# A fused transformer layer on one core: the parts of a block sum in another order, and the casts of a weight pair one quad at a time

## The chip, the cores and the metric

The kernel runs on one core of a Trainium2 chip. The metric is the device time of one execution in microseconds (us); of several runs the median is taken. A measurement of this kernel tells changes of about 0.3% (some 5.5 us) from none.

## The reference, cut to what matters

One layer of a hybrid decoder for 256 positions of width 2048 in float32: a half-step feed-forward block, a mixing block (differential attention beside an mLSTM, with one combined input projection and one output projection), a second half-step feed-forward block, and a final norm. Most of the work is in the feed-forward blocks (inner width 5632):

```
def swiglu(h, w_gate, w_up, w_down):
    return (jax.nn.silu(h @ w_gate) * (h @ w_up)) @ w_down

x = x + 0.5 * swiglu(rmsnorm(x, ffn1_norm[l]), ffn1_w_gate[l], ffn1_w_up[l], ffn1_w_down[l])
...   # h @ w_in, attention and mLSTM, concat @ w_out
x = x + 0.5 * swiglu(rmsnorm(x, ffn2_norm[l]), ffn2_w_gate[l], ffn2_w_up[l], ffn2_w_down[l])
return rmsnorm(x, final_norm)
```

## The kernel before, in words

**A product in three.** A float32 operand is split into a high part, a cast to a rounded format by ScalarE (ACT, line 131, tiles `wh`), and a low part, the difference, by VectorE (DVE, line 132, tiles `wl`). A product of two operands is three matmuls on TensorE (PE): line 180 and line 181 take the weights' high part with the high and the low part of the other operand, line 183 takes the low part `wl`. `mms` issues lines 180 and 181 for all its jobs first and line 183 after them, so `wl` may be a little later than `wh`. `wh` and `wl` have four buffers each.

**Quads.** `Paired` computes two column chunks (512 columns each) of a linear layer at a time, for the two halves of 128 positions. For `ns` of its 2x2 blocks of weights, called quads, it takes seven products instead of eight, by sums of weight blocks and of input blocks. For the rest of the depth it takes plain products (`plain`, tiles `rawp`). Quads are loaded and split two at a time, as pairs of 128x1024 elements; `twos` is the list of them. With `ns` of 5 it is the first pair (quads 0 and 1), the second pair (quads 2 and 3), and a single quad (4), of 128x512 elements. The gate and up projections have `ns` of 5 in 20 passes: 9 in the first feed-forward block, 11 in the second. All other passes have `ns` of 2, 3 or 4, where the list has one pair, a pair and a single quad, or two pairs.

**The stages of a pass.** `leading` loads a pair (POOL's DMA queue, lines 433 and 207; the first passes on SP's), takes the first products (A1), adds weight blocks in place on DVE (line 463), and takes the products with the second sum (S1). Behind S1, `second_sum` adds slot 2 of the raw tile to slot 0: for the pairs by an accumulating DMA from POOL's queue (line 478), for the last entry of the list, the single quad, by DVE (line 480). Between the steps of `leading` run the last steps (`third`) of the pass before. Then `sums` does for each entry of the list the products with the third sum (S2, line 508) from slot 0, loads another block (`late`, SP's queue, line 494), adds that block to slot 0 by an accumulating DMA (line 512, POOL), and takes the block's own products (`bare`, line 500) one entry behind. Behind the last S2, ACT copies the accumulator (`us`, line 486) and DVE subtracts it from another one (line 517). Then come the products with slot 1 (S3, line 523), and in `second` plain products mixed with `both`, which uses slots 0 and 2 of each quad. The order on the engines is that in which the code issues, with loads and splits moved ahead by a priority of 400 instructions (`AHEAD`); copies and additions that empty accumulators are put among the splits by `ahead_of_splits`.

**The output projection.** Its first pass runs with `gently`. In `leading`, after each pair, `flush(1)` issues one piece of pending work; here these are transposes of the mixer's outputs (`y_transposes`, line 1075, which read `yb` or `ya`).

Of the kernel before, what the change touches and what calls it, by code (L numbers as in the profile page):

```python
# [9 lines left out]
F32 = mybir.dt.float32  # L10
# [3 lines left out]
ALU = mybir.AluOpType  # L14
# [45 lines left out]
def tile_trunk_layer(ctx: ExitStack, tc: tile.TileContext, x, xt, par, bias_if, lamv, fnorm,  # L60
                     wg1, wu1, wd1, wqk0, wqk1, wqk2, win, wout, wg2, wu2, wd2, out):
    nc = tc.nc
# [33 lines left out]
    def seeded(which):  # L96
        return ps_acc.tile([P, CW], F32, tag=f"acc{which}", name=nm(f"acc{which}"), bufs=1)
# [26 lines left out]
    def split_gain(src, gcol, hi, lo):  # L124
# [2 lines left out]
        nc.vector.scalar_tensor_tensor(lo, src, prm[:, gcol:gcol + 1], hi.bitcast(F32),  # L127
                                       op0=ALU.mult, op1=ALU.subtract)

    def split(src, hi, lo):  # L130
        return (nc.scalar.copy(hi, src),  # L131
                nc.vector.tensor_tensor(out=lo, in0=src, in1=hi.bitcast(F32), op=ALU.subtract))  # L132

    splits, queued = [], ([], [])

    def after(late, early):

        tc.add_manual_dep(late.ins, early.ins.name,  # L140
                          mybir.DependencyInfo(mybir.DependencyClass.NoSync, mybir.DependencyReason.DATA),
                          reason="order")

    def ahead_of_splits(i, ins, slack=SLACK):
        queued[i].append((len(splits) + slack, ins))

    ahead = ([], [])

    def split_weights(src, hi, lo):
        made = split(src, hi, lo)  # L150
        for late, q, past in zip(made, queued, ahead):
            while q and len(splits) >= q[0][0]:
                past.append(q.pop(0)[1])
            del past[:-3]
            for early in past:
                after(late, early)
        return made


    def pair_tiles(pool, tag, shape):  # L160
        return (pool.tile(shape, F32R, tag=tag + "h", name=nm(tag + "h")),
                pool.tile(shape, F32R, tag=tag + "l", name=nm(tag + "l")))
# [11 lines left out]
    newest = []  # L174

    def mms(jobs):


        for acc, lh, ll, rh, rl, first, last, on in jobs:
            nc.tensor.matmul(acc, lh, rh, start=first, stop=False, skip_group_check=on)  # L180
            nc.tensor.matmul(acc, ll, rh, start=False, stop=False, skip_group_check=on)  # L181
        for acc, lh, ll, rh, rl, first, last, on in jobs:
            newest[:] = [nc.tensor.matmul(acc, lh, rl, start=False, stop=last, skip_group_check=on)]  # L183
# [15 lines left out]
    def flush(n=None):  # L199

        now = pending[:n]
        del pending[:n]
        for f in now:
            f()
# [87 lines left out]
    def chunk_to_xt(c, gbase, xp, ns, now=KD):  # L292


        def run(j):
            tr = ps_tr.tile([P, 2, S], F32, tag="tr", name=nm("tr"))
            for i in range(2):
                for hb in range(NT):
                    nc.tensor.transpose(tr[:, i, hb * P:(hb + 1) * P],
                                        xres[:, hb, (2 * j + i) * P:(2 * j + i + 1) * P], ident)  # L300
            with tc.high_priority(offset=AHEAD):
                if j < ns:
                    sum_pair(xp, j, gained(tr, prm[:, gbase + 2 * j:gbase + 2 * j + 2]), j >= now)
                else:
                    hi, lo = plain_pair(xp, j)
                    for i in range(2):
                        split_gain(tr[:, i, :], gbase + 2 * j + i, hi[:, i, :], lo[:, i, :])

        pending.extend(functools.partial(run, j) for j in (2 * c, 2 * c + 1))
# [14 lines left out]
    def sum_pair(xp, j, g, put_off=False):  # L324
        hi, lo = sum_tiles(xp, j)
        split(g, hi[:, 0:4, :], lo[:, 0:4, :])
        (side.append if put_off else lambda f: f())(functools.partial(sums, g, hi, lo))

    def sums(g, hi, lo):
        s = wk("xsum").rearrange("p (a b) -> p a b", b=P)  # L330
        tt = nc.vector.tensor_tensor
        tt(out=s[:, 0:2, :], in0=g[:, 0:2, :], in1=g[:, 1:4:2, :], op=ALU.subtract)
        tt(out=s[:, 2, :], in0=s[:, 1, :], in1=g[:, 0, :], op=ALU.subtract)
        tt(out=s[:, 3, :], in0=g[:, 2, :], in1=s[:, 2, :], op=ALU.add)
        split(s, hi[:, 4:8, :], lo[:, 4:8, :])
# [18 lines left out]
    def hid_transposes(hs, hid, c, ns):  # L354
        def run(j):
            tr = ps_tr.tile([P, 2, S], F32, tag="tr", name=nm("tr"))
            for i in range(2):
                for hb in range(NT):
                    k = (2 * j + i) % 4
                    nc.tensor.transpose(tr[:, i, hb * P:(hb + 1) * P], hs[hb][:, k * P:(k + 1) * P], ident)  # L360
            if j < ns:
                g = wk("hg")
                act.copy(g, tr.rearrange("p a b -> p (a b)"))
                with tc.high_priority(offset=AHEAD):
                    sum_pair(hid, j, g.rearrange("p (a b) -> p a b", b=P), True)
            else:
                with tc.high_priority(offset=AHEAD):
                    split(tr, *plain_pair(hid, j))

        pending.extend(functools.partial(run, j) for j in (2 * c, 2 * c + 1))  # L370

    def wk(name):
        return work.tile([P, CW], F32, tag="w", name=nm(name))
# [11 lines left out]
    def soon(extra=40):  # L385
        return tc.high_priority(offset=AHEAD + extra)
# [17 lines left out]
    def aside(work):  # L404

        if work:
            work.pop(0)()

    class Paired:
# [28 lines left out]
            self.raws.extend(raw[:, q, :, :] for q in range(len(js)))  # L438
            return raw

        def split_two(self, src):
            with tc.high_priority(offset=AHEAD):
                t = [x[:, 0:src.shape[1], :] for x in pair_tiles(wsp, "w", [P, 2, self.n])]
                splits.append(split_weights(src, *t))
            return t

        def part(self, js, acc, xi, slot, first=False, last=False):

            t = self.split_two(self.twin[js[0]][:, :, slot, :])
            mms([self.job(acc, j, xi, t, i, first and j == 0, last and j == self.ns - 1, not first)  # L450
                 for i, j in enumerate(js)])

# [49 lines left out]
        def sums(self):  # L502

            ds = self.copied(self.d, wk("ds"))
            lates = []
            for js in self.twos:
                lates.append((js, self.late(js)))
                self.part(js, self.x, S2, 0)
                if self.rest[0] // UK not in self.xp:
                    flush(1)  # L510
                with tc.high_priority(offset=AHEAD):
                    nc.gpsimd.dma_start(self.twin[js[0]][:, :, 0, :], lates[-1][1][:, 0:len(js), :],  # L512
                                        accum_op=ALU.add)
                if js[-1] == self.ns - 1:
                    us = self.copied(self.x, wk("us"))
                    with soon():
                        ahead_of_splits(1, nc.vector.tensor_tensor(out=self.d, in0=self.d, in1=us, op=ALU.subtract))
                if len(lates) > 1:
                    self.bare(*lates.pop(0))
            for js, raw in lates:  # L520
                self.bare(js, raw)
            for js in self.twos:
                self.part(js, self.x, S3, 1)
            self.n21 = self.copied(self.x, seeded(N21), SLACK - 2)
            with soon():
                ahead_of_splits(1, nc.vector.tensor_tensor(out=self.x, in0=ds, in1=self.x, op=ALU.subtract))
# [52 lines left out]
    class Chain:  # L579
# [7 lines left out]
        def run(self, p, half, end, last_units=1, gently=False):  # L587

            done = 0
            q = len(p.twos)  # L590
            first = p.leading()
            for i in range(q):
                while done < min(self.steps - 1, -(-(i + 1) * self.steps // (q + 1))):
                    next(self.stream)
                    done += 1
                next(first)
                flush(1)
                aside(side)
            while done < self.steps - 1:
                next(self.stream)  # L600
                done += 1
            next(first, None)
            while done < self.steps:
                next(self.stream)
                done += 1
            self.end()
            p.sums()
            half(p.second(gently))
            self.put(p.third(last_units), len(p.rest), lambda: end(p.accs()))
# [257 lines left out]
    late = {}  # L867
# [263 lines left out]
    for c in (0, 2):  # L1131
        chain.run(Paired(yT, wout[c], wout[c + 1], KD, NP_OUT), functools.partial(finish_out, c),
                  functools.partial(finish_out, c + 1),
                  gently=not c)
# [108 lines left out]
```

## Time and profile before

| what | value |
|---|---|
| median of 3 runs | 1851.19 us (1849.18 to 1855.7) |
| the profiled execution | 1848.02 us, its span 1846.3 us |
| busy in the span | PE 1785.6 us (97%), DVE 1588.7 (86%), ACT 1232.9 (67%), POOL 340.0 (18%) |
| mean granted clock of TensorE | 0.991 |
| traffic | 427.00 MB, 231 GB/s in the mean |

The span runs from the first to the last instruction; the execution's own time is 1.7 us more. A row of the waits reads: who waited, for whom, us in total, times, the longest. A row of the timeline reads: start, duration, engine, line, operation, out<-in, count, and in brackets the engine's idle time before it and what ended it. Matmuls are pipelined: each is shown 0.39 us long where one starts every 0.2275 us.

### The profile page before, as it was taken

The numbers are of one execution on the slowest core, as the hardware profiler recorded it, in microseconds if no ns is written. First come the engines' busy times: TensorE is split into PE (matmuls) and PEld (weight loads), VectorE is DVE, ScalarE is ACT, GpSimd is POOL, SyncE is SP. The second block draws the span as 40 slices with busy tenths as digits, with TensorE's granted clock in tenths as the row PEclk, the third lists the DMA queues.
The fourth block names the chain that finished last, engine by engine and source line by source line (L and its number), as shares of the span: only waits on it lengthen the run. The fifth ranks groups of instructions, "written<-read, shape, count | busy, mean of one in ns | idle before, by whom it ended". The sixth has DMA issues, their size and how long they took to land. (4 is left out here: it accounts for less than half of the span.)

```text
span 1846.3 us, 23318 instructions
## 1 busy us (share of the span) xinstructions
PE 1785.6 (97%) x7942; PEld 1442.7 (78%) x7942; DVE 1588.7 (86%) x1871; ACT 1232.9 (67%) x1659; POOL 340.0 (18%) x444
## 2 busy tenths in 40 slices
PE   9999999999999999999999999999999899999998
PEld 7887777777777788987887887777777677777776
DVE  7888898798888989896788998988898698888988
ACT  7666666566666668776676676675666566666665
POOL 0011221222122211111111001122222222122210
PEclk9999999999999999999999999999999899999999
DMA  9788997888799876576766678887987788798874
GB/s 341 246 240 220 254 266 218 232 260 249 215 238 265 240 246 201 184 227 194 217 193 195 200 211 234 243 240 230 260 253 212 195 258 252 221 238 250 244 242 126
DMA packets 150423, 427.00 MB, mean 231 GB/s; under 512 B 14528, under 2 KB 15600, under 8 KB 150048
## 3 DMA queue, kind: packets, MB, share of 16 engines
q0 software_dynamic: 71472, 191.67, 42.4%
q1 hardware_dynamic: 77680, 231.76, 36.6%
q10 hardware_dynamic: 1152, 2.09, 0.3%
q8 instruction: 62, 1.02, 0.2%
q14 instruction: 57, 0.47, 0.1%
HBM read 349.56 MB, written 2.10 MB: 190 GB/s over the span
## 5 line engine op out<-in xcount | busy, mean ns | idle before, releaser
L131 ACT CAST wh<-raw 128x1024 fp32r<-128x1024 f32 (+1 forms) x593 | 555.4, 943 | 388.2 <-DVE raw L463 94.8
L132 DVE TENSOR_TENSOR wl<-raw,wh 128x1024 fp32r<-128x1024 f32 (+1 forms) x593 | 636.9, 1085 | 181.6 <-ACT wh L131 177.2
L180 PE MATMUL acc<-wh,xs 128*128 128x512 f32 (+2 forms) x924 | 363.9, 394 | 34.0 <-ACT wh L131 33.9
L132 DVE TENSOR_TENSOR wl<-rawp,wh 128x1024 fp32r<-128x1024 f32 (+3 forms) x316 | 373.5, 1195 | 26.6 <-ACT wh L131 22.4
L131 ACT CAST wh<-rawp 128x1024 fp32r<-128x1024 f32 (+3 forms) x316 | 323.2, 1033 | 62.0 <-PE acc L181 34.5
L181 PE MATMUL acc<-wh,xs 128*128 128x512 f32 (+2 forms) x924 | 359.4, 389 | 0.0
L183 PE MATMUL acc<-wl,xs 128*128 128x512 f32 (+2 forms) x924 | 312.0, 394 | 6.9 <-DVE wl L132 5.7
L180 PEld LDWEIGHTS acc<-wh,xs 128*128 128x128 f32 x924 | 175.0, 189 | 79.7 <-ACT wh L131 45.0
L180 PE MATMUL acc<-wh,xt 128*128 128x512 f32 (+2 forms) x592 | 228.6, 387 | 0.0
L181 PE MATMUL acc<-wh,xt 128*128 128x512 f32 (+2 forms) x592 | 228.0, 386 | 0.0
L180 PE MATMUL accn<-wh,xt 128*128 128x512 f32 (+1 forms) x576 | 227.3, 398 | 0.7 <-ACT wh L131 0.6
L181 PE MATMUL accn<-wh,xt 128*128 128x512 f32 (+1 forms) x576 | 224.1, 392 | 0.7
L183 PEld LDWEIGHTS acc<-wl,xs 128*128 128x128 f32 x924 | 171.6, 189 | 55.3 <-DVE wl L132 22.3
L463 DVE TENSOR_TENSOR raw<-raw 128x1024 f32<-128x1024 f32 (+1 forms) x172 | 204.0, 1216 | 7.7 <-DMA raw<-in_wd_dram 6.0
L512 POOL DMA_DIRECT2D raw<-late x104 | 113.9, 1160 | 478.7 <-DVE wl L132 404.4
L181 PEld LDWEIGHTS acc<-wh,xs 128*128 128x128 f32 x924 | 175.1, 190 | 34.0
L183 PE MATMUL acc<-wl,xt 128*128 128x512 f32 (+2 forms) x592 | 165.1, 387 | 3.7 <-DVE wl L132 3.7
L183 PE MATMUL accn<-wl,xt 128*128 128x512 f32 (+1 forms) x576 | 162.0, 389 | 0.2
L180 PE MATMUL accn<-wh,xs 128*128 128x512 f32 (+1 forms) x392 | 155.1, 397 | 1.5 <-ACT wh L131 1.5
L181 PE MATMUL accn<-wh,xs 128*128 128x512 f32 (+1 forms) x392 | 154.0, 394 | 0.0
L183 PE MATMUL accn<-wl,xs 128*128 128x512 f32 (+1 forms) x392 | 139.1, 398 | 2.0 <-DVE wl L132 0.7
L183 PEld LDWEIGHTS acc<-wl,xt 128*128 128x128 f32 x592 | 109.8, 188 | 27.7 <-DVE wl L132 6.2
(229 smaller groups left out, 2052.8 us busy)
## 6 DMA issues: line engine op xcount, KB each, us to landing
rawp<-in_wd_dram SPq DMA_DIRECT2D x88, 512.0 KB, 5.6
raw<-in_wu_dram POOLq DMA_DIRECT2D x80, 512.0 KB, 8.2
rawp<-in_wu_dram SPq DMA_DIRECT2D x74, 512.0 KB, 5.1
rawp<-in_wg_dram SPq DMA_DIRECT2D x70, 512.0 KB, 6.0
raw<-late POOLq DMA_DIRECT2D x67, 512.0 KB, 5.9
raw<-in_wd_dram POOLq DMA_DIRECT2D x60, 512.0 KB, 6.8
rawp<-in_win_dram SPq DMA_DIRECT2D x44, 512.0 KB, 5.0
raw<-raw POOLq DMA_DIRECT2D x43, 512.0 KB, 5.9
```

What stands on the lines that cost most here:

```text
L131: return (nc.scalar.copy(hi, src), nc.vector.tensor_tensor(out=lo, in0=src, in1=hi.bitcast(F32), op=ALU.subtract))
L132: nc.vector.tensor_tensor(out=lo, in0=src, in1=hi.bitcast(F32), op=ALU.subtract))
L180: nc.tensor.matmul(acc, lh, rh, start=first, stop=False, skip_group_check=on)
L181: nc.tensor.matmul(acc, ll, rh, start=False, stop=False, skip_group_check=on)
L183: newest[:] = [nc.tensor.matmul(acc, lh, rl, start=False, stop=last, skip_group_check=on)]
L463: nc.vector.tensor_tensor(out=raw[:, 0:2, :], in0=raw[:, 0:3:2, :], in1=raw[:, 1:2, :].to_broadcast([P, 2, n]), op=ALU.add)
L512: nc.gpsimd.dma_start(self.twin[js[0]][:, :, 0, :], lates[-1][1][:, 0:len(js), :], accum_op=ALU.add)
```

## The change: order and casts

Four edits. In `sums` the list is walked in the order first pair, single quad, second pair; the bare products stay one entry behind, so they come as first pair, single quad, second pair too. For lists of one or two entries the order is what it was. In `part`, that is, for the pairs of A1, S1, S2 and S3, ACT casts a pair in two instructions of one quad each, and DVE still subtracts it in one; single quads, plain units, bare products and `both` are split as before. In the first pass of the output projection, `flush(1)` in `leading` is ordered behind the newest matmul.

```diff
+    def lo_part(src, hi, lo):
+        return nc.vector.tensor_tensor(out=lo, in0=src, in1=hi.bitcast(F32), op=ALU.subtract)
...
-    def split_weights(src, hi, lo):
-        made = split(src, hi, lo)
-        for late, q, past in zip(made, queued, ahead):
+    def split_weights(src, hi, lo, apart=False):
+        first = [nc.scalar.copy(hi[:, q, :], src[:, q, :]) for q in range(src.shape[1])] if apart else []
+        made = (first[-1], lo_part(src, hi, lo)) if apart else split(src, hi, lo)
+        for late, q, past in zip(first[:-1] + list(made), [queued[0]] * len(first[:-1]) + list(queued),
+                                 [ahead[0]] * len(first[:-1]) + list(ahead)):
...
         def part(self, js, acc, xi, slot, first=False, last=False):
-            t = self.split_two(self.twin[js[0]][:, :, slot, :])
+            t = self.split_two(self.twin[js[0]][:, :, slot, :], True)
...
-            for js in self.twos:
+            order = self.twos[:1] + self.twos[2:] + self.twos[1:2]
+            for js in order:
                 lates.append((js, self.late(js)))
                 self.part(js, self.x, S2, 0)
...
-                if js[-1] == self.ns - 1:
+                if js == order[-1]:
...
                 next(first)
-                flush(1)
+                if gently:
+                    with tc.issue_after(newest[0].ins):
+                        flush(1)
+                else:
+                    flush(1)
```

More of the change, by code (lines that the diff above doesn't have):

```diff
@@ L128, in split_gain @@
                                        op0=ALU.mult, op1=ALU.subtract)
+    def lo_part(src, hi, lo):
+        return nc.vector.tensor_tensor(out=lo, in0=src, in1=hi.bitcast(F32), op=ALU.subtract)
     def split(src, hi, lo):
-        return (nc.scalar.copy(hi, src),
-                nc.vector.tensor_tensor(out=lo, in0=src, in1=hi.bitcast(F32), op=ALU.subtract))
+        return nc.scalar.copy(hi, src), lo_part(src, hi, lo)
     splits, queued = [], ([], [])
@@ L439, in load, with split_two @@
             return raw
-        def split_two(self, src):
+        def split_two(self, src, apart=False):
             with tc.high_priority(offset=AHEAD):
                 t = [x[:, 0:src.shape[1], :] for x in pair_tiles(wsp, "w", [P, 2, self.n])]
-                splits.append(split_weights(src, *t))
+                splits.append(split_weights(src, *t, apart))
             return t
         def part(self, js, acc, xi, slot, first=False, last=False):
-            t = self.split_two(self.twin[js[0]][:, :, slot, :])
+            t = self.split_two(self.twin[js[0]][:, :, slot, :], True)
             mms([self.job(acc, j, xi, t, i, first and j == 0, last and j == self.ns - 1, not first)
```

## The prediction

> **What bounds the kernel now.** I read the page's first part, then the waits, then the timeline of one pass on each engine, then the stretches of all passes.
>
> ```profile
> span 1846.3 us, 23318 instructions
> PE 1785.6 (97%) x7942; PEld 1442.7 (78%) x7942; DVE 1588.7 (86%) x1871; ACT 1232.9 (67%) x1659; POOL 340.0 (18%) x444
> ```
>
> PE is busy for 97% of the span, so only its idle time, slow starts and lowered clock can be won. DVE, at 86%, is not far behind. The waits say what PE waits for:
>
> ```profile
> PE acc L180 <- ACT wh L131: 33.9, 23, 3.3
> PE acc L183 <- DVE wl L132: 9.4, 14, 1.4
> ACT wh L131 <- DMA raw<-raw: 76.0, 23, 5.5
> DVE wl L132 <- ACT wh L131: 201.6, 179, 5.8
> ```
>
> PE waits 23 times for a cast, and ACT waits 23 times for `raw<-raw`, the accumulating DMA of line 478. One pass shows that these are the same event. PE, around the third sum (S2):
>
> ```profile
> 429.57 0.39 PE L180 MATMUL acc<-wh,xs 128*128 128x512 f32 x1
> ...
> 430.48 0.61 PE L183 MATMUL acc<-wl,xs 128*128 128x512 f32 x2
> 432.75 0.50 PE L180 MATMUL acc<-wh,xs 128*128 128x512 f32 x1 [1.66 <-ACT wh L131]
> ...
> 434.58 0.39 PE L180 MATMUL accn<-wh,xs 128*128 128x512 f32 x1
> ...
> 436.38 0.39 PE L180 MATMUL acc<-wh,xs 128*128 128x512 f32 x1
> ...
> 442.29 0.39 PE L183 MATMUL acc<-wl,xs 128*128 128x512 f32 x1
> ```
>
> From 429.57 to 430.48 four matmuls start: one each 0.2275 us, so a pair (six) takes 1.365 and a single quad 0.68. The first pair's S2 ends at 430.93 (430.48 and two more starts). The second pair's S2 starts at 432.75, 1.82 late; its six take 1.83 (0.47 too long), the six bare ones behind it 1.80 (0.43 too long). This pass loses 2.72 us. ACT, POOL and SP in the same place:
>
> ```profile
> 427.24 0.57 ACT L486 COPY ds<-acc 128x512 f32<-128x512 f32 x1
> 431.66 1.04 ACT L131 CAST wh<-raw 128x1024 fp32r<-128x1024 f32 x1 [3.84 <-DMA raw<-raw]
> ...
> 433.57 0.61 ACT L131 CAST wh<-raw 128x512 fp32r<-128x512 f32 x1
> 434.08 1.56 ACT L131 CAST wh<-late 128x1024 fp32r<-128x1024 f32 x2
> ```
> ```profile
> 425.63 1.21 POOL L478 DMA_DIRECT2D raw<-raw  x1 [4.07 <-DVE wl L132]
> ```
> ```profile
> 400.18 13.15 SPq L494 DMA_DIRECT2D late<-in_wg_dram  x3
> ```
>
> POOL issues the second pair's sum at 425.63, as soon as DVE is through with S1 of that pair; it lands 6.0 later, at 431.66. ACT has been idle for 3.84 and casts; PE follows. The single quad's cast (433.57) stands in the queue behind, though its sum is made by DVE and needs no DMA. Line 480 in the next view has made it by 427.73:
>
> ```profile
> 427.04 0.69 DVE L480 TENSOR_TENSOR raw<-raw 128x512 f32<-128x512 f32 x1
> 427.64 1.22 DVE L132 TENSOR_TENSOR wl<-raw,wh 128x1024 fp32r<-128x1024 f32 x1
> 428.78 0.74 DVE L382 SCALAR_TENSOR_TENSOR sg<-acc,rstd,sg 128x512 f32<-128x512 f32 x1
> 432.73 1.23 DVE L132 TENSOR_TENSOR wl<-raw,wh 128x1024 fp32r<-128x1024 f32 x1 [3.21 <-ACT wh L131]
> 433.88 0.75 DVE L382 SCALAR_TENSOR_TENSOR sg<-acc,rstd,sg 128x512 f32<-128x512 f32 x1
> 434.54 1.22 DVE L132 TENSOR_TENSOR wl<-late,wh 128x1024 fp32r<-128x1024 f32 x1
> 435.67 0.69 DVE L132 TENSOR_TENSOR wl<-raw,wh 128x512 fp32r<-128x512 f32 x1
> ...
> 438.01 1.22 DVE L132 TENSOR_TENSOR wl<-raw,wh 128x1024 fp32r<-128x1024 f32 x1
> 439.14 0.69 DVE L517 TENSOR_TENSOR acc<-acc,us 128x512 f32<-128x512 f32 x1
> 439.74 1.22 DVE L132 TENSOR_TENSOR wl<-raw,wh 128x1024 fp32r<-128x1024 f32 x1
> ```
>
> DVE too is idle for 3.21 and then works without a gap to the end of S3: behind the stall DVE sets the pace, and this limits the gain. A pair costs it 1.13 (434.54 to 435.67), a single quad 0.60. All 20 passes with five quads have this place; one of them, the first, has no wait. For the other 19, PE in the 8 us behind the first pair's S2, one stretch each (first, some of the middle, last, and the sum over 19):
>
> ```profile
> 209.21:217.21 8.00, 6.58 (x26) 1.00 1.00 180
> ...
> 430.93:438.93 8.00, 6.14 (x25) 1.00 0.93 184
> ...
> 1353.68:1361.68 8.00, 6.30 (x20) 0.79 0.93 187
> 1449.88:1457.88 8.00, 4.84 (x12) 0.67 0.76 146
> ...
> 1691.12:1699.12 8.00, 6.14 (x19) 0.79 0.93 186
> 1736.25:1744.25 8.00, 6.28 (x20) 0.79 0.94 188
> sum 152.00, PE 121.55; mean PE 6.40
> ```
>
> The columns are length, PE busy, matmuls, granted clock, DMA share, GB/s. Idle: 152.00 - 121.55 = 30.5 us. At 430.93 the idle part is 1.86 of the 2.72 lost; the other 0.86 are starts further apart. I take 0.82 for the mean (two passes wait less): 19 x 0.82 = 15.5. The clock: 8 x 0.21 in three stretches and 8 x 0.33 in one, 7.7. Together the place costs **53.7 us**.
>
> On the clock the Trainium skill (TensorE: Matmul & The Clock Gate, HAM oscillation) says that it halves after an idle window of about 3.4 us. By that rule only the pass at 1449.88 (3.16 idle) could lose clock here, the 7.7 would mostly have other causes, and the sum below would be some 5 smaller. The stretches at 1353.68, 1691.12 and 1736.25, with 1.7 to 1.9 idle in 8 us and 0.79 granted, speak against the rule as the only cause.
>
> **The change part by part.**
>
> *The order.* In the pass above, ACT is free at 427.81. It casts the single quad (0.51 to the next start, from 433.57 to 434.08) and the first pair's bare block by 429.4; their buffers were freed by S1. The late blocks are long there: SP issued three by 413.3. Moving the single quad ahead moves its late load and its accumulating DMA ahead of the second pair's on SP and POOL too. The second pair's late block becomes the third load; with the 6.0 of the sum's DMA it lands by 419.5, and its first user is behind 433. On POOL the single quad's issue takes 1.2 in a queue that then waits for the second pair's DVE anyway, and slot 0 is not read again before `both`, beyond S3 (442.5). I cost these at nothing; if that cover went, the wait would show in `both`.
>
> PE: single quad 430.93 to 431.61, bare products to 432.98, then the second pair, **2.05 later** than asked for before. Its first cast ends at 431.66 + 0.62 = 432.28: no wait. DVE can start its subtraction when both casts are done, 432.79, and ends at 434.01; line 183 wants it at 432.98 + 0.91 = 433.89. That is 0.17 late with the signal. In the 3.21 that DVE was idle it now does the single quad (0.60), the bare block (1.13) and, if it stands there, the second line 382 (0.66). Behind it I walk on by the same durations: if line 382 comes early, DVE is in time for the rest, and S3 ends at 439.97 instead of 442.52, a gain of 2.55 of the 2.72. If line 382 stays behind the second pair, all that follows is 0.66 later, which PE feels as some 0.5: gain 2.05. So 0.17 to 0.67 stays per pass; Nothing in the trace tells which it will be, so I take the middle, 0.42: 19 x 0.42 = 8.0. The pass at 1449.88 waited 3.16 idle, over 2.05 + 0.17 by about 1; I leave 1.7 there with its restart. Won: 53.7 - 8.0 - 1.7 = **44.0**. Bounds: 53.7 from above, and from below what DVE allows if nothing of the idle time is filled but the 1.73 of two subtractions, less 0.67 of new waiting: 19 x 1.06 = 20.1.
>
> Does DVE have that time over a whole pass?
>
> ```profile
> 386.10:429.60 43.50, 41.96 (x187) 33.73 (x186) 40.14 (x46) 30.32 (x38) 10.08 (x14) 1.00 0.87 248
> ```
>
> This is one of the fullest (PE, PEld, DVE, ACT, POOL busy): 40.14 of 43.50. Less 2.1 to 2.3 the pass is 41.2 to 41.4, DVE at 97%. It fits, barely; the DMA share rises from 0.87 to 0.92.
>
> *The casts.*
>
> ```profile
> L131 ACT CAST wh<-raw 128x1024 fp32r<-128x1024 f32 x441 | 462.7, 1051 | 288.7 <-DMA raw<-raw 76.0 <-DVE raw L463 62.9 <-PE accn L181 58.1
> L131 ACT CAST wh<-raw 128x512 fp32r<-128x512 f32 x146 | 90.6, 620 | 98.4 <-DVE raw L463 30.9 <-DMA raw<-in_wd_dram 19.2 <-DMA raw<-in_wg_dram 18.0
> ```
>
> By the code 272 pairs go through `part` (8 in each of 20 passes, 112 elsewhere). A pair's cast is done after 0.51 + 0.62 = 1.13 instead of 1.05: DVE gets it 0.08 later, PE its first quad 0.43 earlier. ACT is busy up to 272 x 0.19 = 52 us more (2 x 620 - 1051), 22 by the starts, out of 613 idle. In the place above both effects are counted. Elsewhere the waits of PE for a first cast (23 less the 19 of S2, so four) gain 0.43 each and DVE's 14 lose 0.08 each: **0.6** won. From below, if all 179 waits of DVE for a cast grew by 0.08 to 0.19 and reached PE, 14 to 34 lost; nearest is the near end, since PE's waits for DVE are 14 and not 179. Per-quad casts also let S1's cast begin after the first of two additions (line 463); the row shows 62.9 of such idle time, but DVE, not ACT, is the pace there, so I count no gain.
>
> The Trainium skill (Perfetto Trace Analysis, Optimizing Scalar/DVE Operations) speaks against this edit: an instruction of ScalarE on SBUF pays about 93 ns, and grouping raises throughput. Its figure gives an estimate of 25 us for 272, beside my 22; it would be lost only where ACT is saturated, which at 67% it isn't.
>
> *The flush.*
>
> ```profile
> 1012.54 0.30 PE L1075 MATMUL tr<-ident,yb 128*128 128x128 f32 x1 [1.11 <-DVE yb L397]
> ```
>
> The transposes stand before matmuls that could run. Behind the newest matmul they don't hold PE: up to 1.1 won; if something else is late there, 0; from below, -1.1, if the transposes' users then wait as long as PE did. Only matmuls that are ready are put ahead of them, so I take a value near the gain, **0.8**.
>
> *Sum.* 44.0 + 0.6 + 0.8 = 45.4. The profiled execution took 1848.02: 1802.6. The median of the runs stands 3.2 above it (1851.19): **1806**.
>
> **The rivals.**
>
> *DVE becomes the bound.* For it: DVE's gapless run behind the stall and the 97% above. Then the low end of the order's gain holds, with the clock: 20.1 + 7.7 = 28, so 1823. Against: 3.21 of idle time at the very place.
>
> *The wait only moves.* If ACT's queue still has the second pair's cast in front, or PE waits as long at the next step, nothing is won: 1850. For it: the landing itself doesn't come earlier. Against: single quad, bare block and their subtractions are ready by 431.
>
> *Slower.* Split casts where DVE has no slack: each of its 179 waits grows by 0.08 to 0.19 and the order brings nothing, since DVE's work is the bound throughout: 1851 + 14 to 34, so 1865 to 1885. It decides from the point where DVE's idle time in a pass (3.4 of 43.5) is no longer slack. Against: that idle time is one piece, before the second pair.
>
> *More than all of it.* Fewer waits also keep the clock up elsewhere (the longest wait, 3.3, is in A1): below 1796.
>
> **How the numbers follow.** Forecast, 1796 to 1816: 0.60. DVE as the bound, 1816 to 1832: 0.22. Moved wait: 0.06. Slower: 0.06. More: 0.06. The range 1796 to 1832 leaves out 0.18. Faster by over 0.3% (5.5 us, about what a measurement can tell): 0.60 + 0.22 + 0.06 = 0.88; same 0.06; slower 0.06.
>
> **What would show it.** Right: ACT's waits for `raw<-raw` keep some time, but PE's for casts fall from 33.9 to below 12 and the 8 us stretches hold 31 or more matmuls; line 180 of the second pair follows the bare products without a gap; DVE's longest gap in a pass shrinks from 3.2 to 1 or 1.5; PE's waits for `wl` rise from 9.4 to some 15. Wrong: waits for `wl` above 25 (DVE is the bound), or a new wait in front of the single quad or in `both`. A landing later than 6 us after the issue, from denser DMA traffic, would bring the old wait back.

## The result, and the profile after

The kernel after takes 1808.2 us in the median of 4 runs (1806.17 to 1812.71), the kernel before beside it 1853.45: a ratio of 0.9758, with a 95% interval of 0.9724 to 0.9792. The prediction said 1806. The profiled execution took 1809.75 us, 38.3 less than the 1848.02 of before.

The page's first part, of the kernel after:

```profile
span 1808.0 us, 23592 instructions
PE 1769.6 (98%) x7942; PEld 1439.5 (80%) x7942; DVE 1587.3 (88%) x1871; ACT 1254.6 (69%) x1931; POOL 340.3 (19%) x444
```

PE and DVE do the same work in 38 us less. ACT has 272 more instructions (1931 against 1659) and is busy 21.7 longer, as the starts had let expect (22). The mean granted clock went from 0.991 to 0.995.

The rows of its waits that stand against the four of before (total, times, longest). In this kernel line 152 is the cast of a pair, 134 any other cast, 131 the subtraction; lines 184 and 187 are the former 180 and 183:

```profile
DVE wl L131 <- ACT wh L152: 91.1, 86, 6.7
DVE wl L131 <- ACT wh L134: 78.4, 91, 2.6
...
ACT wh L152 <- DMA raw<-raw: 30.3, 20, 3.4
...
PE acc L187 <- DVE wl L131: 14.2, 26, 1.1
...
PE acc L184 <- ACT wh L152: 9.4, 6, 3.9
```

PE's waits for a cast fell from 33.9 (23 times) to 9.4 (6 times), ACT's for the accumulating DMA from 76.0 to 30.3; PE's waits for `wl` rose from 9.4 to 14.2. These are the marks that the prediction set: below 12, some left, some 15.

The pass that the prediction walked through stands 5.3 us earlier in this trace. PE:

```profile
425.22 0.62 PE L187 MATMUL acc<-wl,xs 128*128 128x512 f32 x2
425.67 0.39 PE L184 MATMUL acc<-wh,xs 128*128 128x512 f32 x1
...
426.35 0.39 PE L184 MATMUL accn<-wh,xs 128*128 128x512 f32 x1
...
427.71 0.39 PE L184 MATMUL acc<-wh,xs 128*128 128x512 f32 x1
...
428.96 0.74 PE L187 MATMUL acc<-wl,xs 128*128 128x512 f32 x2 [0.18 <-DVE wl L131]
...
431.63 0.39 PE L184 MATMUL acc<-wh,xs 128*128 128x512 f32 x1
```

The first pair's S2 ends at 425.67, where the single quad begins; the bare products follow at 426.35 and the second pair at 427.71, with no gap. Line 187 waits 0.18 (the prediction had 0.17), and S3 begins at 431.63. The 24 matmuls from 425.67 to S3 need 24 x 0.2275 = 5.46 and take 5.96: 0.50 is left of the 2.72 that this pass lost. The engines around it, DVE, ACT and POOL:

```profile
426.02 0.74 DVE L386 SCALAR_TENSOR_TENSOR sg<-acc,rstd,sg 128x512 f32<-128x512 f32 x1
427.68 1.23 DVE L131 TENSOR_TENSOR wl<-raw,wh 128x1024 fp32r<-128x1024 f32 x1 [0.92 <-ACT wh L152]
```
```profile
426.51 1.14 ACT L152 CAST wh<-raw 128x512 fp32r<-128x512 f32 x2 [2.11 <-PE acc L187]
```

DVE's idle piece shrank from 3.21 to 0.92, a little below the forecast 1 to 1.5. The second line 386 (382 before) stands early, at 426.02, ahead of the second pair's subtraction: the better of the two cases that the prediction left open. ACT's cast of the second pair now ends 427.65, just as PE comes.

The stretches of 8 us behind the first pair's S2, for the 20 passes (columns as before: length, PE, PEld, DVE, ACT, POOL, clock, DMA share, GB/s):

```profile
103.77:111.77 8.00, 8.00 (x37) 6.63 (x36) 7.63 (x9) 6.61 (x10) 1.20 (x1) 1.00 1.04 207
...
425.67:433.67 8.00, 7.82 (x34) 6.12 (x33) 7.08 (x9) 7.16 (x12) 1.67 (x2) 1.00 1.06 217
...
1428.37:1436.37 8.00, 6.86 (x29) 4.93 (x28) 5.94 (x8) 5.85 (x11) 2.06 (x2) 1.00 1.01 203
...
sum 160.00, PE 156.72 PEld 123.01 DVE 145.91 ACT 144.12 POOL 39.12; mean PE 7.84 PEld 6.15 DVE 7.30 ACT 7.21 POOL 1.96
```

Without the first row, 19 passes: 152.00 - 148.72 = 3.3 us idle, against 30.5, and the clock is 1.00 in each. One stretch alone holds fewer than 31 matmuls, the one at 1428.37.

**Where the time went, by stages.** I add up, over all matmuls, by how much each start lies later than the one before it plus its own length (0.2275 us for 512 columns), and put the excess to the stage of the later one. The slower clock is in it.

| kernel | S2 and bare | S1 | A1 | third (`third`) | plain and `both` behind S3 |
|---|---|---|---|---|---|
| before | 54.1 | 10.0 | 8.4 | 6.3 | 12.9 |
| after | 11.8 | 15.2 | 10.3 | 4.6 | 10.0 |

S2 and bare won 42.3; S1 and A1 gave 7.1 back. Here and below, such a sum comes from one profiled execution, which can lie some us off the median of its kernel: that of before is 5.4 below (1848.02 against 1853.45), that of after 1.6 above, e1's 6.4 above, e2's 4.6 above, e11's 3.3 below. A difference of a few us between two sums is not shown by them alone.

### The profile page after: what moved, and what is told of

Same layout as the page of the kernel before. It is cut to its first block, busy times and chain, and to the rows that moved or that the text cites. A ratio compares the mean times of both kernels' runs of the same rounds, so it can differ in the third digit from the quotient of the medians.

```text
span 1808.0 us, 23592 instructions
## 1 busy us (share of the span) xinstructions
PE 1769.6 (98%) x7942; PEld 1439.5 (80%) x7942; DVE 1587.3 (88%) x1871; ACT 1254.6 (69%) x1931; POOL 340.3 (19%) x444
## 5 line engine op out<-in xcount | busy, mean ns | idle before, releaser
L152 ACT CAST wh<-raw 128x512 fp32r<-128x512 f32 x688 | 398.8, 618 | 275.6 <-DVE raw L467 79.4
L134 ACT CAST wh<-raw 128x1024 fp32r<-128x1024 f32 (+2 forms) x177 | 184.8, 1045 | 67.0 <-PE accn L185 45.7
L184 PE MATMUL accn<-wh,xs 128*128 128x512 f32 (+1 forms) x392 | 153.1, 391 | 2.0 <-ACT wh L134 2.0
L185 PE MATMUL accn<-wh,xs 128*128 128x512 f32 (+1 forms) x392 | 152.1, 389 | 0.0
```

The source lines that it names most:

```text
L134: return nc.scalar.copy(hi, src), lo_part(src, hi, lo)
L152: first = [nc.scalar.copy(hi[:, q, :], src[:, q, :]) for q in range(src.shape[1])] if apart else []
```

## The experiments

| run | kernel | median, us | ratio to before, 95% |
|---|---|---|---|
| e1_order | the order alone | 1806.25 | 0.9758, 0.9737 to 0.9780 |
| e2_casts | the casts alone | 1855.15 | 1.0016, 1.0003 to 1.0029 |
| e3_dvesum | old order, second pair's sum by DVE | 1812.97 | 0.9787, 0.9769 to 0.9805 |
| e4_cover1 | after, with 0.68 us of cover only | 1836.66 | 0.9923, 0.9905 to 0.9941 |
| e5_early | order, with 2.73 us of cover | 1810.96 | 0.9779, 0.9759 to 0.9800 |
| e6_order_dvesum | order, and the sum by DVE | 1805.88 | 0.9749, 0.9733 to 0.9764 |
| e7_noadd | order, one addition a pass left out | 1796.78 | 0.9696, 0.9675 to 0.9717 |
| e8_soonboth | order, `both` one step earlier | 1812.76 | 0.9785, 0.9763 to 0.9806 |
| e9_soonboth_full | after, `both` one step earlier | 1820.95 | 0.9815, 0.9787 to 0.9843 |
| e10_defer | order, slot 1 added behind S1 | 1804.63 | 0.9737, 0.9724 to 0.9750 |
| e11_defer_s2 | order, slot 1 added behind S2 | 1805.95 | 0.9742, 0.9726 to 0.9757 |

**e1_order: the order alone.**

```diff
-            for js in self.twos:
+            order = self.twos[:1] + self.twos[2:] + self.twos[1:2]
+            for js in order:
...
-                if js[-1] == self.ns - 1:
+                if js == order[-1]:
```

> The new order alone, every pair cast in one instruction as before. Theory (the wait is for the landing of line 478, and the 2.05 us of other products cover it): nearly the whole gain, ratio 0.973 to 0.979 to the kernel before, about 1808 us; PE's wait for casts below 14 us. The second pair's subtraction can start 0.08 us earlier than with split casts, so it may even be a little better than the full change. Rival (the gain needs the first quad's cast 0.43 us earlier): 19 x 0.43 = 8 us less gain, ratio about 0.980 to 0.985.

0.9758, the ratio of the whole change. S2 and bare fell to 7.3 us of excess, S1 rose to 18.5. The order alone brings what the change brings.

**e2_casts: the split casts alone**, that is, the diff of the change without its part in `sums` and without the flush.

> The split casts alone, in the old order. Theory: a pair's six products end when its subtraction comes, and that comes 0.08 us later than before, so PE's first product behind the wait starts 0.43 us earlier but nothing ends earlier: ratio 0.997 to 1.003, PE's wait for casts down by 19 x 0.43 = 8 us, its wait for wl up by as much. Rival (the earlier first product counts): 8 to 10 us faster, ratio 0.995. Rival (ACT or DVE have no slack): 179 waits longer by 0.08 to 0.19, ratio 1.008 to 1.018.

Slower by 0.16%, 3 us, with an interval that just leaves out no change and lies within what a measurement tells. Its waits:

```profile
ACT wh L152 <- DMA raw<-raw: 76.5, 24, 5.5
...
PE acc L184 <- ACT wh L152: 31.1, 22, 4.6
...
PE acc L187 <- DVE wl L131: 18.7, 34, 1.2
```

PE's waits for casts went down by 2.8 (33.9 to 31.1), not by the 8 that was expected, and its waits for `wl` up by 9.3 (9.4 to 18.7, 14 times to 34). One place shows why:

```profile
435.60 0.61 PE L187 MATMUL acc<-wl,xs 128*128 128x512 f32 x2
437.31 0.50 PE L184 MATMUL acc<-wh,xs 128*128 128x512 f32 x1 [1.10 <-ACT wh L152]
...
439.09 0.73 PE L187 MATMUL acc<-wl,xs 128*128 128x512 f32 x2 [0.53 <-DVE wl L131]
439.66 0.39 PE L184 MATMUL accn<-wh,xs 128*128 128x512 f32 x1
```

PE begins the second pair earlier (1.10 idle instead of 1.66) and then waits 0.53 at its low part. From the end of the first pair's S2 (436.05) to the bare products it is 3.61, before it was 434.58 - 430.93 = 3.65. The end of the chain is DVE's subtraction, which needs both casts, so a first cast that is early only moves the wait. In 17 of the 19 places PE waits at the low part in this way, 0.52 to 0.54 each; in the trace of before it does so in none. These rows tell the kind of loss, not its size: this execution took 1859.73, 4.6 more than e2's median, at the lowest granted clock of its twelve (0.986).

**e3_dvesum: another way to take the late DMA away.** The old order; DVE adds the second pair's slot 2 to slot 0, so the wait for that DMA can't occur.

```diff
-                if self.by_dma and js != self.twos[-1]:
+                if self.by_dma and js != self.twos[-1] and not (len(self.twos) == 3 and js == self.twos[1]):
```

> The kernel before in its old order, but the second pair's sum for S2 (slot 0 plus slot 2) is made by DVE (128x1024, 1.22 us, 1.13 by the starts) instead of by the accumulating DMA, in the 20 passes of five quads. Theory (PE waits for the landing): the wait in front of the second pair goes, PE's wait for casts falls from 33.9 to below 14 us; DVE gets 20 x 1.13 = 23 us more in a stretch where it has no gap, so part of the 53.7 us comes back as waits for wl: 1815 to 1830 us, ratio 0.980 to 0.989. Rival (DVE is the bound anyway): 1851 or slower, up to 1874, ratio 1.000 to 1.012.

0.9787, better than the expected 0.980 to 0.989. S2 alone, without the bare products, fell from some 43 to 0.7 us of excess; ACT's waits for `raw<-raw` fell from 76.0 to 4.9. That the accumulating DMA was the cause of the lost time in S2 is thereby shown without moving any product. The price was DVE's:

```profile
PE 1773.3 (98%) x7942; PEld 1436.3 (79%) x7942; DVE 1609.2 (89%) x1891; ACT 1235.3 (68%) x1659; POOL 315.0 (17%) x424
```

DVE is busy 20.5 longer (1609.2 - 1588.7), and the run is some 5 to 7 us behind e1_order, with intervals that overlap. In its trace the excess of `third` stands at some 15 us, against 6.3 before. So 20 us of DVE work ahead of S2 did not become 20 us of time: DVE is not the bound of the whole kernel.

**e4_cover1: the new order with less cover.** The bare products of the first pair come behind the second pair's S2, so that only the single quad (0.68 us) stands ahead of it instead of 2.05.

```diff
-                if len(lates) > 1:
+                if len(lates) > (2 if len(order) == 3 else 1):
```

> The changed kernel, but the first pair's bare products come behind the second pair's S2 instead of ahead of it: only the single quad (0.68 us) covers the landing instead of 2.05. Theory (the cover is what counts, in us): the second pair is asked for 1.37 us earlier in 19 passes, so up to 26 us come back; 1825 to 1836 us, ratio 0.985 to 0.992. Rival (what counts is that ready work stands ahead in ACT's queue at all): like the changed kernel, 0.976.

0.9923, just above the expected 0.985 to 0.992. Its waits:

```profile
ACT wh L152 <- DMA raw<-raw: 64.2, 26, 5.0
...
PE acc L187 <- DVE wl L131: 18.5, 33, 1.2
PE acc L184 <- ACT wh L152: 17.2, 21, 3.8
```

S2 and bare keep 42.0 us of excess. By the ratios, 0.68 us of cover won 0.0077 x 1852 = 14 us and 2.05 won 0.0242 x 1852 = 45, that is 0.7 and 2.2 in each of 20 passes; between the profiled executions it was 12.4 and 38.3, that is 0.6 and 1.9. The gain goes with the cover, as the walk had it.

**e5_early: more cover.** With the order alone, the single quad's bare products also go ahead of the second pair: 2.05 + 0.68.

```diff
                 lates.append((js, self.late(js)))
+                if len(order) == 3 and js == order[-1]:
+                    self.bare(*lates.pop(0))
                 self.part(js, self.x, S2, 0)
```

> The new order alone, casts as before, and in the passes of five quads the single quad's bare products also ahead of the second pair's S2: cover 2.73 us instead of 2.05. Theory (what is left in S2, about 6 us in the run with the order alone, is a landing later than the cover): S2's loss falls below 3 us, ratio 0.972 to 0.976, 1801 to 1806 us. Rival (what is left is set by DVE's run from A1 to S1, or the copy us, now only 1.36 us ahead of its users, makes S3 wait): same as the order alone, 0.976, or slower by up to 20 x 0.3 = 6 us.

S2 alone, without the bare products, fell further, from some 6 us of excess to 2.1, but the time did not: 0.9779, where e1_order has 0.9758, with intervals that overlap. The expected gain (0.972 to 0.976) did not come; the rival holds. S1 stayed at 18.5, A1 at 11.0. At 2.05 the cover was as good as enough.

**e6_order_dvesum: both remedies.** The edits of e1_order and e3_dvesum together.

> The new order alone and the second pair's sum by DVE as well, so that S2 waits for no landing and DVE has 20 x 1.13 = 23 us more work in the stretch from S1 to S2. Theory (PE is the bound, DVE has some slack left): between the order alone and the DVE sum alone, ratio 0.975 to 0.980. Rival (with the order DVE is at its bound, 97% of a full pass): most of the 23 us come back, 0.983 to 0.988.

1805.88, with S2 alone at 2.0: within the intervals no different from the order alone, though DVE has 20 us more to do (1608.3). Either remedy takes the same loss away; the second finds nothing left.

**e7_noadd: less DVE work between landing and S1.** With the order edit, in the 20 passes the addition behind the single quad's A1 products (line 463) is left out.

```diff
-                    for j in js:
+                    for j in (js if len(self.twos) < 3 or len(js) == 2 else ()):
```

> The new order alone, and in the 20 passes of five quads the single quad's weight sums in leading (line 463, one 128x1024 addition, 1.22 us of DVE between A1 and S1) are left out, so its products of the first and second sums use plain blocks. This tells what sets PE's loss in S1, 18.5 us in the run with the order alone. Theory (from the landing of a raw load on, DVE works without a gap to S1, and its work there sets the pace): 20 x 1.13 us less work in that run, S1's loss falls below 10 us, ratio 0.968 to 0.972. Rival (the landing of the loads sets it, DVE follows): S1's loss stays above 14 us, ratio 0.973 to 0.977.

1796.8, 0.6% below e1_order. S1's excess fell from 18.5 to 7.2, by as much as the time (11.3 against some 11.5). So what is left in S1 hangs on DVE's work there. The timeline of such a place in the kernel after, DVE and then PE:

```profile
1455.18 2.36 DVE L467 TENSOR_TENSOR raw<-raw 128x1024 f32<-128x1024 f32 x2
...
1460.97 2.35 DVE L467 TENSOR_TENSOR raw<-raw 128x1024 f32<-128x1024 f32 x2
1463.24 0.68 DVE L131 TENSOR_TENSOR wl<-raw,wh 128x512 fp32r<-128x512 f32 x1
1463.96 1.23 DVE L467 TENSOR_TENSOR raw<-raw 128x1024 f32<-128x1024 f32 x1
1465.10 1.82 DVE L131 TENSOR_TENSOR wl<-raw,wh 128x1024 fp32r<-128x1024 f32 x2
```
```profile
1466.38 0.73 PE L187 MATMUL acc<-wl,xs 128*128 128x512 f32 x2 [0.98 <-DVE wl L131]
```

DVE runs without a wait from 1455.18 on; the addition that e7 leaves out is that at 1463.96, and PE waits 0.98 for the subtraction behind it.

**e8_soonboth and e9_soonboth_full: loads a step earlier.** `both` empties the raw tiles, and the next pass's loads wait for that. The edit on the order alone (e8) and on the kernel after (e9):

```diff
-                if 0 < i <= self.ns:
-                    both(i - 1)
+                if i < self.ns:
+                    both(i)
```

> The new order alone, and in second every both(j) one plain unit (2.73 us) earlier, so that the raw tiles are free, and the next pass's loads are issued, up to 2.73 us earlier against PE. Theory (behind the change the next bound is the distance from both over the load's 6 to 10 us landing and DVE's run to S1): the waits in A1 in front of two passes (3.0 each, and the lowered clock behind) shrink, A1 and S1 lose less than 18 us instead of 28.6, ratio 0.966 to 0.972, 1790 to 1801 us. Rival (the loads are late for the DMA engines' bandwidth or POOL's queue, not for their issue): unchanged, 0.974 to 0.978. Against it: both then waits for the accumulating DMA of line 512.

> The changed kernel with every both(j) one plain unit earlier. Theory: like the order alone with that edit, since the casts change nothing beyond 0.2%: the same ratio within 0.003. Rival (split casts help once S1's chain from load to product is what PE waits for, by 0.43 us a step): 0.003 or more better than the order alone with it.

Neither won what was expected of it. e8 has 0.9785 beside the 0.9758 of the order alone, with intervals that overlap; e9 has 0.9815 beside the 0.9758 of the kernel after, with intervals that meet only at their ends, so it is probably some 0.6% slower. A1's excess did fall (e1_order 10.1, e8 7.7; after 10.3, e9 5.8), but the plain products and `both` behind S3 went from 12.8 to 22.4 in e8 and from 10.0 to 27.0 in e9. A place in e8, ACT and then PE:

```profile
297.26 1.04 ACT L131 CAST wh<-raw 128x1024 fp32r<-128x1024 f32 x1 [2.43 <-DMA raw<-late]
298.21 0.58 ACT L486 COPY accn<-acc 128x512 f32<-128x512 f32 x1
```
```profile
298.84 0.50 PE L180 MATMUL accn<-wh,xt 128*128 128x512 f32 x1 [1.42 <-ACT accn L486]
```

The first cast of `both` waits 2.43 for the accumulating DMA of `late` (line 512 of the kernel before), the copy that PE needs stands behind it in ACT's queue, and PE waits 1.42. It is the kind of stall that the change removed in S2, at another place.

**e10_defer and e11_defer_s2: the same additions, later.** Of the additions behind A1, slot 0 is read by S1 and slot 1 only by S3. e10 leaves slot 0 in place and adds slot 1 behind S1, in `second_sum`; e11 adds it behind each entry's S2, in `sums`. This holds for all passes with quads, not only for the 20, and both have the order edit. The first two pieces of e10's edit:

```diff
-                    for j in js:
-                        raw = self.raws[j]
-                        nc.vector.tensor_tensor(out=raw[:, 0:2, :], in0=raw[:, 0:3:2, :],
-                                                in1=raw[:, 1:2, :].to_broadcast([P, 2, n]), op=ALU.add)
+                    raw = self.twin[js[0]]
+                    nc.vector.tensor_tensor(out=raw[:, :, 0, :], in0=raw[:, :, 0, :], in1=raw[:, :, 1, :], op=ALU.add)
...
+                nc.vector.tensor_tensor(out=raw[:, :, 1, :], in0=raw[:, :, 1, :], in1=raw[:, :, 2, :], op=ALU.add)
```

> The order edit, and of the additions behind A1 only slot 0 (which S1 reads) stays there; slot 1 (read by S3) is added behind S1, by an instruction of its own. The work is the same: two instructions of 1.22 us a pair as before, and for a single quad two of 0.68 instead of one of 1.22. Theory (what is left in S1, 18.5 us with the order edit, is DVE's gapless run from the landing of the raw load to S1): the second pair's S1 subtraction comes 1.13 + 0.6 us earlier in the 20 passes, as in the run without the single quad's addition (which came to 1796.8), at no work left out: S1 falls to 7 to 10 us and the time to 1796 to 1801. Rival 1 (the run gained by having less DVE work at all): the additions only come later, S1's gain returns as waits for wl in S2 and in the third products, 1804 to 1809. Rival 2 (they delay the subtraction of the first pair's S2, which has had no wait): slower than the order edit, 1809 to 1820.

> As the run beside it, but slot 1 is added only behind each entry's S2, in sums. Theory: S1 is freed of all three additions (2.9 us in a pass), so S1 falls to 5 us or below; but DVE had only about 0.9 us idle left ahead of the second pair's S2, so some 2 us of work in a pass now stands in front of that pair's subtraction and the bare products: S2 and bare rise by up to 1 us in a pass, 1800 to 1815. If additions in S2 cost nothing, because the DMA of that place is what DVE waits for, 1793 to 1798. Rival: as for the run beside it, no gain, 1804 to 1809.

S1's excess fell to 8.4 in e10 and 6.4 in e11, as the theory had it, but the time hardly moved: 0.9737 and 0.9742, against 0.9758 of the order alone, with overlapping intervals. In e10 the products of `third` went from 7.1 to 17.5. PE there:

```profile
1650.91 0.73 PE L183 MATMUL acc<-wl,xs 128*128 128x512 f32 x2 [0.20 <-DVE wl L132]
1653.85 0.73 PE L183 MATMUL acc<-wl,xt 128*128 128x512 f32 x2 [0.61 <-DVE wl L132]
```

The first row is S1; the second is the plain product behind it, which in e10 waits 0.61 for its own `wl`, because the deferred addition stands ahead of that subtraction. Rival 1 of the expectation holds for e10: S1 won 10.1 and `third` lost 10.4, so in this stretch the amount of DVE work counts, not its order. For e11 it holds by the time alone. In its trace `third` rose to some 10 only, and S1's gain of 12.1 is not found again in the other stages; but its execution and e1's differ by as much (1802.70 and 1812.70) while their medians agree. Where e11's gain went stays open. e10 has the lowest time of the runs that leave nothing out, but it can't be told from the order alone or from the kernel after.

## Why the prediction was right, and where it wasn't

**The cost of the place, 53.7:** the excess of S2 and bare was 54.1. Right.

**The order, 44.0, with 9.7 left:** S2 and bare won 42.3, with 11.8 left. Mechanism and size hold: two kernels that take the wait away by different means (e1, e3) both win 2.1 to 2.4%, and less cover wins less (e4). In the pass shown, both bounds of the remaining loss (line 183 late by 0.17; line 382 early or late) were well set, and line 382 came early. Part of what is left belongs to the split casts: in the trace after, eight of the second pairs wait for `wl`, 0.18 to 0.52 each, in e1's none, and there S2 and bare keep 7.3. The pass that had waited longest, to which 1.7 was left, still waits in the trace after: 0.62 for a cast and 0.52 for `wl` there, at 1431.19 and 1432.97.

**Costed at nothing, not so:** the prediction said that a wait would show in `both` if the cover went. It didn't show there (`both` and the plain products beside it: 12.9 before, 10.0 after) but one stage on. S1 and A1 gave back 7.1 us. In S1 (5.2 of it), with PE no longer late, DVE's run through the additions comes due earlier, as e7 shows. In A1 (1.9) it is another wait, for a load. The longest of these, in the kernel after, PE and ACT:

```profile
329.20 0.79 PE L184 MATMUL acc<-wh,xs 128*128 128x512 f32 x1 [3.87 <-ACT wh L152]
```
```profile
328.53 2.70 ACT L152 CAST wh<-raw 128x512 fp32r<-128x512 f32 x5 [6.87 <-DMA raw<-in_wg_dram]
```

PE waits 3.87 for the first cast of a pass, and that for its raw load. Such a wait stood in the trace before too (the 3.3 in A1), and the order doesn't touch it; what made A1's waits longer by 1.9, no run tells.

**The casts, 0.6 won:** alone they lose some 3 us (e2); on top of the order they change nothing that can be told (0.9758 twice). The step that failed is the multiplication: "14 waits lose 0.08 each". Their number rose from 14 to 34, because PE, let in earlier by the first cast, met DVE later at the same pair. The 0.43 that PE won at each first cast was counted as time, though the subtraction, which needs both casts, ends the pair. The Trainium skill (Perfetto Trace Analysis, Optimizing Scalar/DVE Operations) speaks for grouping instructions where the engine is saturated, and says that breaking them up may help where it isn't and holds up another engine. The prediction read the first half of this only; the case here is the second, since ACT at 69% had room for the 21.7 us and PE waited for its casts. Yet e2 shows no gain, because the subtraction behind the casts ends last.

**The flush, 0.8 won:** nothing. The row in the kernel after:

```profile
1002.70 0.30 PE L1084 MATMUL tr<-ident,yb 128*128 128x128 f32 x1 [1.12 <-DVE yb L401]
```

It was 1.11 before. With and without this edit the instructions stand in the same order on all five engines, so a run of it alone would have been a run of the same program. The step that failed is "the transposes stand before matmuls that could run"; they already stood behind the newest one, and what they wait for is DVE's `yb`.

**The sum, 45.4:** 38.3 between the two profiled executions, 45 between the medians of the runs (1853.45 - 1808.2), 38.6 to 51.2 by the interval. Within the two traces the sum is 7 us too high: S2 and bare won 42.3, S1 and A1 gave 7.1 back, the last two columns of the table won 4.6, and 1.5 was lost elsewhere. That the medians agree with 45.4 so well is luck: the profiled execution of before lies 5.4 below its median here and that of after 1.6 above, which just makes up for it.

**The rivals.** *DVE becomes the bound* (1823): not for the kernel (e3 and e6 add 20 us of DVE work and lose at most a few), but for the stretch from A1 to the product behind S1 it is (e7 won 11 us there, e10 only moved it). *The wait only moves* (1850): not in this edit; it is what e2, e8 and e9 did. *Slower by split casts* (1865 to 1885): the mechanism is real, but its price is 3 us (0.6 to 5.4 by the interval), since most of DVE's waits never reach PE. *More than all of it* (below 1796): the clock did improve, from 0.991 to 0.995, but not that far.

## What to carry to other kernels

When an engine waits for a transfer that can't be issued earlier, look for work of the same queue that is ready and doesn't need it, and put in front as much as the wait is long: two microseconds of cover won two microseconds in each pass, a third of it a third, and more than the wait nothing. An instruction made earlier is worth something only if it feeds the last input of its consumer; ask which of several inputs ends last before splitting one. And when a stage is freed, work out the stage behind it under the new times: work that is only put off there (e10) comes due again one product later.

## What the runs showed of the hardware

The granted clock fell to one half after waits much shorter than expected. In the traces the halved stretches begin on a grid of 3.41 us, and follow a piece of this grid in which PE had little to do. Pairs of neighbouring pieces in the trace of before (length, PE with its matmuls, PEld, DVE, ACT, POOL, clock, DMA share, GB/s):

```profile
251.10:254.50 3.40, 1.98 (x8) 0.99 (x6) 1.26 (x2) 2.34 (x3) 0.00 (x0) 1.00 1.03 249
254.50:257.90 3.40, 3.22 (x13) 2.37 (x14) 3.40 (x4) 2.81 (x5) 1.91 (x2) 1.00 0.78 139
...
1353.60:1357.00 3.40, 1.70 (x7) 0.94 (x6) 1.55 (x2) 2.63 (x4) 0.02 (x1) 1.00 1.06 264
1357.00:1360.40 3.40, 3.40 (x9) 2.62 (x9) 3.40 (x5) 2.26 (x3) 2.05 (x2) 0.50 0.73 127
...
1735.90:1739.30 3.40, 1.70 (x7) 0.76 (x5) 1.26 (x2) 2.33 (x3) 0.00 (x0) 1.00 1.03 252
1739.30:1742.70 3.40, 3.38 (x8) 2.70 (x9) 3.40 (x4) 2.06 (x4) 1.92 (x2) 0.50 0.77 136
```

PE busy for 1.70 of 3.40, with one wait of 1.63 and 1.65, is followed by a piece at 0.50; 1.98 of 3.40, with a wait of 1.38, was not. By this busy time the line is not sharp: another piece of the same trace with 1.78 was not followed by a slow one and one with 2.08 was. It becomes sharp when each matmul counts with the 0.2275 us to the next start instead of the 0.39 that it is shown long; the two pieces at 1.70 are then filled to 0.36 and 0.38, the one at 1.98 to 0.45. In all 13 traces together, without the pieces that are at half rate themselves, each of the 39 pieces filled to 0.385 or less was followed by half rate, 8 of the 13 between 0.385 and 0.42 were, and none of the some 6700 filled to more.

The Trainium skill (TensorE: Matmul & The Clock Gate, Part 1) says that the gate watches a free-running window of 4096 cycles; the grid agrees with that. The rule of the Trainium skill (TensorE: Matmul & The Clock Gate, HAM oscillation), no idle gaps of more than about 3.4 us, does not tell the whole of it: a piece that was six tenths idle was enough. So a wait of under two microseconds costs itself and, by where it falls on the grid, up to 1.7 us more (half of 3.41). The grid lies elsewhere in each execution: counted from the span's start its pieces begin 1.91 behind a multiple of 3.413 in the trace of before and 0.87 behind in that of after, so the same wait can cost clock in one execution and none in the next. That the fill is what counts is read from these traces; no run varied it alone.
